# Samples among the last attention chunks, a third cache buffer, the sink's share by a small exp, rope's sum read from PSUM, and a scheduler that knows a shared port

## The chip, the cores and the metric

The kernel runs on one core of one Trainium2 chip. The metric is device time in microseconds (us); lower is better. The engines are TensorE (PE in the profile), VectorE (DVE), ScalarE (ACT), GpSimd (POOL) and SyncE (SP, which here only issues DMA). SBUF is the core's memory of 128 partitions, PSUM the accumulators in eight banks, which PE writes.

## The reference, cut to what matters

One inference step of a model of two layers: 512 prompt tokens, and eight samples of eight new tokens each (64 more), width 1024, all in float32.

```python
# layer 0: recurrent block (RNN), then SwiGLU          (FFN0)
x = x + g1 * recurrent_block(modulate(rms_norm(x, g), sh1, sc1))
x = x + g2 * swiglu(modulate(rms_norm(x, g), sh2, sc2))
# keys and values, once, from the stream after layer 0 (kv)
k, v = split(modulate(rms_norm(x, g), shk, sck) @ w_kv);  k = rope(k)
# layer 1: sliding-window attention with sinks, then SwiGLU (FFN1)
q = rope(h @ w_q)                                     # 16 heads of 64, 4 of k and v
s = (q @ k.T) * HEAD_DIM ** -0.5                      # in blocks of 128, window 128
m = maximum(max(s), sink)
e = exp(s - m)
p = e / (sum(e) + exp(sink - m))
x = x + g1 * ((p @ v) @ w_o)
x = x + g2 * swiglu(...)
y = rms_norm(x, final_g)
```

`apply_partial_rope` turns the first 16 elements of each head: `x1*cos - x2*sin`, `x2*cos + x1*sin`. A sample attends to its cache of 128 keys and to its own eight tokens.

## The kernel before, in words

**Data.** The 576 tokens are handled in two halves, A (`h = 0`) and B (`h = 1`), each of 256 prompt tokens and four samples of eight: `HC` = 288 columns. Features lie on partitions, tokens on columns. A product in float32 is made of three fp32r products, with the weights and the activations split in a high and a low part. One output tile of 128 features is 24 matmuls of 128x288 into one PSUM bank; an evacuation function then takes it from there.

**Order.** The code does not issue instructions. Each call on an engine is recorded (`Engine.record`, `Recorder.add`), which is why every instruction of the profile has the line L422. `Recorder.schedule` (L211) then simulates the engines with an estimated cost for each operation (L373 on) and the handover times of `DELAY` (L355), and takes on each engine, among the next 24 steps that are ready, the one with the smallest start plus 0.75 of its priority. Priority is the program order, within a window `WIN`. A switch of ACT's function table costs 2500 in that key. What comes out is a fixed order for each engine. Tiles come from pools: six PSUM banks `mm`, two `ada`, and the SBUF pools `sl` (37), `ta` (7), `tb` (8), `td` (4) of a few hundred columns each; a step that needs a tile waits for one to come free.

**Stages.** RNN, its output projection, FFN0, kv, attention, FFN1, final norm. Within the attention stage the list `ATT` (L53) sets the program order: `q6B` is the q projection of chunk 6 in half B, `a6B` the attention of that chunk (two heads by two blocks of 128 queries), `s1B` the attention of the second sample of half B, `fB` the end of attention (`attn_fin`), `o0B` an output projection. What comes behind `o2A` follows in its natural order.

**A q projection** ends in `evac_q` (L1492) with `rope` (L1426): DVE shuffles the bank into `t`, DVE multiplies the bank by the cosine table into `u`, POOL multiplies `t` by the sine table, and POOL adds both into the tile of q. The projection of keys, `evac_k`, uses `rope` as well, with two sums, for prompt and samples.

**An attention chunk** (`attn_chunk`, L1530) makes the scores on PE in two banks. DVE adds the mask and takes the row maximum into `ta`/`tb`; POOL writes the sink times 8 into one more column; ACT takes the exp over the scores and that column, with the sum; DVE the reciprocal; DVE and POOL scale two of the four blocks each. `second()`, which runs behind the next chunk's first part, transposes them on PE, copies them to `td` and multiplies with the values into an `ada` bank.

**A sample** (`attn_sample`, L1605) loads its cache rows (two DMAs on SP) into one of two buffers, transposes the keys on PE, and goes through the same steps with 160 columns. Its product with the cached values adds into a bank that the four samples of a half share (`OS`); the fourth one adds the product with the samples' own values.

Of the kernel before, what the change touches and what calls it, by code (L numbers as in the profile page):

```python
# [15 lines left out]
AF = mybir.ActivationFunctionType  # L16
# [36 lines left out]
ATT = ("q0A q1A a0A q0B q2A q1B a1A a0B q3A a1B q4A q2B a2A q3B a2B q5A q4B a3A q6A a3B a4A q5B "  # L53
       "a4B a5A q7A q6B a5B s0A a6A q7B s1A s2A s3A fA a7A a7B a6B s0B o0A s1B o1A s2B s3B fB o2A")
# [30 lines left out]
class Op:  # L85
    __slots__ = ("i", "prio", "eng", "emit", "cost", "func", "preds", "succ", "npred", "ready", "allocs", "start", "end", "done", "lat", "tiles", "_n")
# [42 lines left out]
class Recorder:  # L129
# [11 lines left out]
    @contextmanager  # L141
    def together(self):

        self.batch = []
        yield
        b, self.batch = self.batch, None

        def emit():
            for x in b:
                x[1]()  # L150

        self.add(b[0][0], emit, sum(x[2] for x in b), [y for x in b for y in x[3]], [y for x in b for y in x[4]])
# [22 lines left out]
    def add(self, eng, emit, cost, outs, ins, func=None, lat=0):  # L175
        if self.batch is not None:
            self.batch.append((eng, emit, cost, outs, ins))
            return
# [3 lines left out]
        op.eng, op.emit, op.cost, op.func, op.lat = eng, emit, cost, func, lat  # L182
        op.preds, op.succ, op.allocs, op.tiles = set(), [], [], set()
# [27 lines left out]
    def schedule(self):  # L211
# [18 lines left out]
        cold = 0.0  # L230
        pos = {n: j for k in self.order for j, n in enumerate(self.order[k])}
# [40 lines left out]
        while n_left:  # L272
# [7 lines left out]
            for e in engs:  # L280
# [3 lines left out]
                for pr, i, op in avail[e]:  # L284
# [10 lines left out]
                    s = max(f, op.ready, at)  # L295
                    sw = e == "ACT" and op.func and op.func not in FREE_FUNCS and (table[0] is None or op.func not in TABLES[table[0]][1])
# [25 lines left out]
            cost = op.cost  # L322
            if e == "PE":
                if s - free[e] > 3400:
                    cold = s + 3400
                if s < cold:
                    cost *= 2
# [36 lines left out]
class Engine:  # L364
# [8 lines left out]
    def record(self, name, args, kw):  # L373
# [11 lines left out]
        func, lat = None, 0  # L385
        if name == "matmul":
# [5 lines left out]
            if dt == F32 and 64 in (first.ap[0][1], args[1].ap[0][1]) and n >= P:  # L392

                cost = n * 2 / 2.4 + 20
            if first.ap[0][1] == 32 and args[1].ap[0][1] == P and n >= P:
                cost = n / 2.4 + 30 if dt == F32 else n / 9.6 + 15
        elif name == "transpose":
# [24 lines left out]
        self.rec.add(eng, lambda: getattr(obj, name)(*map(real, args), **{k: real(v) for k, v in kw.items()}), cost, outs, ins, func, lat)  # L422
# [26 lines left out]
def trunk_kernel(ctx, tc, a):  # L449
# [956 lines left out]
    def sink_setup():  # L1406
        sinks, sink8, nsink, sinkS = snk[:, 0:16], snk[:, 16:32], snk[:, 32:48], snk[:, 48:51]
        A["sink8"], A["nsink"], A["sinkS"] = sink8, nsink, sinkS
        sk = a["attn_sinks"][0]
        Q.dma_start(sinks.rearrange("p (g j l) -> p g j l", g=2, j=2), sk.partition_broadcast(P).rearrange("p (g j l) -> p g j l", g=2, j=2))  # L1410
# [3 lines left out]
        sv = sinks.rearrange("p (g j l) -> p g l j", g=2, j=2)  # L1414
        V.tensor_scalar(sink8.rearrange("p (g l j) -> p g l j", g=2, l=4)[:, 0], sv[:, 0], 8.0, None, ALU.mult)
        V.tensor_scalar(sink8.rearrange("p (g l j) -> p g l j", g=2, l=4)[:, 1], sv[:, 1], 8.0, None, ALU.mult)
        V.tensor_scalar(nsink.rearrange("p (g l j) -> p g l j", g=2, l=4)[:, 0], sv[:, 0], -1.0, None, ALU.mult)
        V.tensor_scalar(nsink.rearrange("p (g l j) -> p g l j", g=2, l=4)[:, 1], sv[:, 1], -1.0, None, ALU.mult)
# [111 lines left out]
    def attn_chunk(c):  # L1530
# [3 lines left out]
        def run(h):  # L1534
# [12 lines left out]
            masks, sink8, nsink = A["masks"], A["sink8"], A["nsink"]  # L1547
            for b, W in enumerate(wide):
                i = slice(2 * b, 2 * b + 2)
                for j in range(2):  # L1550
# [3 lines left out]
                    G.tensor_copy(y[:, W : W + 1], sink8[:, 2 * c + j : 2 * c + j + 1])  # L1554
                V.scalar_tensor_tensor(nm[:, i], mx[:, i], -0.125, nsink[:, 2 * c : 2 * c + 2], ALU.mult, ALU.min)
                for j in range(2):
                    y = e[b][j].f[:, 0 : W + 1]
                    S.activation(y, y, AF.Exp, bias=nm[:, 2 * b + j : 2 * b + j + 1], scale=0.125, accum_out=den[:, 2 * b + j : 2 * b + j + 1])
            V.reciprocal(rd, den)
            for b, W in enumerate(wide):  # L1560
                for j in range(2):
                    y, r = e[b][j].f[:, 0:W], rd[:, 2 * b + j : 2 * b + j + 1]
                    if b == j:
                        V.tensor_scalar(y, y, r, None, ALU.mult)
                    else:
                        G.tensor_tensor(y, y, r.to_broadcast([P, W]), ALU.mult)
# [394 lines left out]
```

## Time and profile before

| | |
|---|---|
| runs | 1310.57, 1307.85, 1308.14 us; median 1308.14 |
| profiled execution | 1308.17 us, of it the trace's span 1306.4 us |
| mean granted clock of PE | 0.986 |
| matmul records | 9532 |
| ACT busy, share | 643.8 us, 49% |
| HBM read, written | 160.85 MB, 4.87 MB |

The profile is one execution of the program. A row of a group names line, engine, operation, the output's and the input's tile, and the shapes; buffer numbers are left out there. `wh` are weights and other large tiles, `reg` constant areas, `h` the activations that a projection reads, `sl`, `ta`, `tb`, `td` the pools above. The granted clock is a share of full speed. A row of the timeline is one instruction or a group of like ones, with the idle time of its engine ahead of it and the instruction that ended it. PE's records overlap a little, so their starts tell more than their lengths.

### The profile page before, as it was taken

The numbers are of one execution on the slowest core, as the hardware profiler recorded it, in microseconds if no ns is written. First come the engines' busy times: TensorE is split into PE (matmuls) and PEld (weight loads), VectorE is DVE, ScalarE is ACT, GpSimd is POOL, SyncE is SP. The second block draws the span as 40 slices with busy tenths as digits, with TensorE's granted clock in tenths as the row PEclk, the third lists the DMA queues.
The fourth block names the chain that finished last, engine by engine and source line by source line (L and its number), as shares of the span: only waits on it lengthen the run. The fifth ranks groups of instructions, "written<-read, shape, count | busy, mean of one in ns | idle before, by whom it ended". The sixth has DMA issues, their size and how long they took to land. (4 is left out here: it accounts for less than half of the span.)

```text
span 1306.4 us, 25463 instructions
## 1 busy us (share of the span) xinstructions
PE 1256.6 (96%) x9532; PEld 1174.2 (90%) x9532; DVE 917.1 (70%) x2106; ACT 643.8 (49%) x1419; POOL 527.8 (40%) x813
## 2 busy tenths in 40 slices
PE   6998989999999999999998998999999999999997
PEld 5787889998999999999988886899999999999997
DVE  6986885697467547746688776457975875785767
ACT  4786873574245325424457555437642552552433
POOL 3465451224255145325246678201323633542422
PEclk8998999999999999999999999899999999999999
DMA  9963536325644735554342120233142332233232
GB/s 306 311 207 113 188 124 187 109 93 182 206 148 135 241 122 161 170 186 130 113 97 63 43 66 15 82 106 125 49 130 65 98 98 81 82 105 90 65 98 73
DMA packets 223981, 165.40 MB, mean 127 GB/s; under 512 B 23757, under 2 KB 209065, under 8 KB 223826
## 3 DMA queue, kind: packets, MB, share of 16 engines
q1 hardware_dynamic: 223410, 163.45, 41.1%
q8 instruction: 75, 1.23, 0.4%
q14 instruction: 48, 0.39, 0.1%
q0 software_dynamic: 448, 0.32, 0.1%
HBM read 160.85 MB, written 4.87 MB: 127 GB/s over the span
## 5 line engine op out<-in xcount | busy, mean ns | idle before, releaser
L422 PE MATMUL mm<-h,wh 128*128 128x288 f32 x4128 | 598.3, 299 | 10.8 <-ACT ta L422 3.7
L422 PEld LDWEIGHTS mm<-h,wh 128*128 128x128 f32 x4128 | 561.9, 189 | 32.7 <-issue 11.1
L422 PE MATMUL mm<-sl,wh 128*128 128x288 f32 x3218 | 460.0, 296 | 2.1 <-DVE wh L422 2.1
L422 PEld LDWEIGHTS mm<-sl,wh 128*128 128x128 f32 x3218 | 436.5, 188 | 8.8 <-PE ada L422 3.4
L422 ACT CAST wh<-raw 128x512 fp32r<-128x512 f32 (+2 forms) x388 | 266.9, 710 | 302.6 <-PE mm L422 231.6
L422 DVE TENSOR_TENSOR wh<-raw,wh 128x512 fp32r<-128x512 f32 (+2 forms) x388 | 358.3, 945 | 55.4 <-ACT wh L422 51.7
L422 POOL TENSOR_TENSOR raw<-raw 128x512 f32<-128x512 f32 x76 | 111.3, 1466 | 189.0 <-DVE wh L422 188.8
L422 DVE SCALAR_TENSOR_TENSOR x<-mm,mods,x 128x256 f32<-128x256 f32 x160 | 77.1, 482 | 147.8 <-PE mm L422 147.5
L422 POOL TENSOR_TENSOR x<-x,ta 128x32 f32<-128x32 f32 x152 | 57.6, 379 | 298.0 <-DVE ta L422 297.8
L422 POOL TENSOR_TENSOR raw<-raw,raw 128x512 f32<-128x512 f32 x76 | 111.8, 1473 | 3.3
L422 PE MATMUL mm<-tb,wh 128*128 128x288 f32 (+1 forms) x488 | 90.2, 298 | 6.1 <-POOL tb L422 2.8
L422 PEld LDWEIGHTS mm<-tb,wh 128*128 128x128 f32 x488 | 72.6, 188 | 10.9 <-POOL tb L422 3.5
L422 POOL TENSOR_TENSOR td<-td,td 128x288 f32<-128x288 f32 x38 | 33.1, 872 | 111.1 <-ACT td L422 105.7
L422 ACT COPY td<-mm 128x256 f32<-128x256 f32 (+1 forms) x102 | 34.1, 353 | 45.8 <-PE mm L422 41.1
L422 PE MATMUL mm<-ta,wh 128*128 128x288 f32 (+1 forms) x254 | 56.2, 298 | 0.0
L422 DVE TENSOR_TENSOR td<-mm,td 128x288 f32<-128x288 f32 x76 | 33.5, 452 | 31.7 <-PE mm L422 31.3
L422 ACT ACTIVATE ta<-x 128x288 f32<-128x288 f32 x56 | 24.8, 444 | 56.5 <-POOL x L422 53.4
L422 PE MATMUL ada<-reg,cz 128*32 128x512 f32 (+1 forms) x448 | 49.5, 553 | 0.0
L422 DVE TENSOR_TENSOR sl<-ta,sl 128x288 fp32r<-128x288 f32 x54 | 43.4, 806 | 3.8 <-ACT sl L422 3.4
L422 PEld LDWEIGHTS mm<-ta,wh 128*128 128x128 f32 x254 | 41.6, 188 | 2.5 <-issue 0.8
L422 ACT COPY ta<-mm 128x288 f32<-128x288 f32 (+1 forms) x50 | 18.9, 378 | 36.2 <-PE mm L422 36.1
L422 DVE TENSOR_TENSOR sl<-td,sl 128x288 fp32r<-128x288 f32 x50 | 34.3, 686 | 3.1 <-ACT sl L422 3.1
(198 smaller groups left out, 1287.0 us busy)
## 6 DMA issues: line engine op xcount, KB each, us to landing
raw<-in_ffn_w_in_dram SPq DMA_DIRECT2D x88, 512.0 KB
reg<-in_ada_w_dram SPq DMA_DIRECT2D x80, 512.0 KB
raw<-in_ffn_w_out_dram SPq DMA_DIRECT2D x48, 384.0 KB
raw<-in_rnn_w_in_dram SPq DMA_DIRECT2D x16, 512.0 KB
reg<-in_kv_ada_w_dram SPq DMA_DIRECT2D x16, 512.0 KB
wh<-in_ada_w_dram SPq DMA_DIRECT2D x24, 256.0 KB
raw<-in_rnn_w_out_dram SPq DMA_DIRECT2D x8, 512.0 KB
raw<-in_ffn_w_out_dram SPq DMA_DIRECT2D x16, 256.0 KB
```

The lines of the kernel that those rows point to most:

```text
L422: self.rec.add(eng, lambda: getattr(obj, name)(*map(real, args), **{k: real(v) for k, v in kw.items()}), cost, outs, ins, func, lat)
```

## The change

It has six parts.

1. `ATT`: a chunk follows its q projection one projection later than before in most places, and the samples stand among the last chunks.
2. Three cache buffers in place of two: the sample with `b % 3 == 2` uses the free half of `KT[1]` (`wh277` below).
3. The sink's share of the sum is no longer a column of the exp: DVE adds `nm + sink` (two values for each block), ACT takes one small exp over the four, DVE adds it to the sums. Of the four blocks ACT scales two (`j == 0`), POOL and DVE one each. The samples keep the column.
4. `rope` multiplies the bank by the cosines in place, and DVE, not POOL, adds POOL's product to it, out of the bank. The tile `u` is gone.
5. The scheduler holds that operations of POOL and those of DVE that read two SBUF inputs exclude each other (`port`), that PE needs 100 ns between matmuls of different shapes of array use (`mode`), and some costs are changed.
6. The setup of the sinks is written for part 3.

```diff
-ATT = ("q0A q1A a0A q0B q2A q1B a1A a0B q3A a1B q4A q2B a2A q3B a2B q5A q4B a3A q6A a3B a4A q5B "
-       "a4B a5A q7A q6B a5B s0A a6A q7B s1A s2A s3A fA a7A a7B a6B s0B o0A s1B o1A s2B s3B fB o2A")
+ATT = ("q0A q1A a0A q0B q2A a1A q1B a0B q3A a2A q2B a1B q4A a3A q3B a2B q5A a4A q4B a3B q6A a5A q5B a4B q7A a6A s0A q6B a5B s1A "
+       "a7A s2A q7B s3A s0B a6B fA s1B o0A s2B a7B s3B o1A fB o2A")
...
                     s = max(f, op.ready, at)
+                    if op.port:
+                        s = max(s, port - 130)
+                    if e == "PE" and op.mode != mode:
+                        s = max(s, f + 100)
...
+            if op.port:
+                port = s + cost
+            if e == "PE":
+                mode = op.mode
...
+        wide = [x for x in ins if not _is_psum(x) and not str(x.space).endswith("DRAM") and (_free(x) > 1 or f == 1)]
+        port = eng == "POOL" and name != "dma_start" and bool(wide) or eng == "DVE" and not ps_ and (len(wide) > 1 or name == "tensor_scalar" and f > 1)
...
-            cost, lat = (460.0 if eng == "SP" else 1020.0), n * 4 / 360.0 + 5
+            cost, lat = (460.0 if eng == "SP" else 1020.0), n * 4 / 335.0 + 5
...
+            elif name == "tensor_tensor_scan":
+                cost = 70 + 2.1 * f
...
-                cost = 67 + (1.2 if name == "tensor_tensor" and not ps_ and f >= 288 else 1.0417) * f + (61 if scal and name == "scalar_tensor_tensor" else 0)
+                cost = 67 + 1.0417 * f + (61 if scal and name == "scalar_tensor_tensor" else 0)
...
-                cost = 145 + (165 if ALU.pow in vals else 2.6) * f
+                cost = 150 + (165 if ALU.pow in vals else 2.4) * f
...
     def rope(h, o, outs):
-        t, u = ta(), tb()
+        t = ta()
         tabs = A["tabs"]
         V.stream_shuffle(t.f[:, 0:HC], o[:, 0:HC], SHUF)
-        V.tensor_tensor(u.f[:, 0:HC], o[:, 0:HC], tabs[h][:, 0, :], ALU.mult)
         G.tensor_tensor(t.f[:, 0:HC], t.f[:, 0:HC], tabs[h][:, 1, :], ALU.mult)
+        V.tensor_tensor(o[:, 0:HC], o[:, 0:HC], tabs[h][:, 0, :], ALU.mult)
         for cs, dst in outs:
-            G.tensor_tensor(dst, u.f[:, cs], t.f[:, cs], ALU.add)
+            V.tensor_tensor(dst, o[:, cs], t.f[:, cs], ALU.add)
         t.done()
-        u.done()
...
-                    G.tensor_copy(y[:, W : W + 1], sink8[:, 2 * c + j : 2 * c + j + 1])
                 V.scalar_tensor_tensor(nm[:, i], mx[:, i], -0.125, nsink[:, 2 * c : 2 * c + 2], ALU.mult, ALU.min)
+                V.tensor_tensor(mx[:, i], nm[:, i], sinks[:, 2 * c : 2 * c + 2], ALU.add)
                 for j in range(2):
-                    y = e[b][j].f[:, 0 : W + 1]
+                    y = e[b][j].f[:, 0:W]
                     S.activation(y, y, AF.Exp, bias=nm[:, 2 * b + j : 2 * b + j + 1], scale=0.125, accum_out=den[:, 2 * b + j : 2 * b + j + 1])
+            S.activation(mx, mx, AF.Exp)
+            V.tensor_tensor(den, den, mx, ALU.add)
             V.reciprocal(rd, den)
             for b, W in enumerate(wide):
                 for j in range(2):
                     y, r = e[b][j].f[:, 0:W], rd[:, 2 * b + j : 2 * b + j + 1]
-                    if b == j:
+                    if j == 0:
+                        S.activation(y, y, AF.Copy, scale=r)
+                    elif b == 0:
+                        G.tensor_tensor(y, y, r.to_broadcast([P, W]), ALU.mult)
+                    else:
                         V.tensor_scalar(y, y, r, None, ALU.mult)
-                    else:
-                        G.tensor_tensor(y, y, r.to_broadcast([P, W]), ALU.mult)
...
-            ck, cv = cache[:, b % 2, 0, :], cache[:, b % 2, 1, :]
+            ck, cv = [KT[1].f[:, 512 + 256 * i : 768 + 256 * i] if b % 3 == 2 else cache[:, b % 3, i, :] for i in range(2)]
```

The program has 8972 matmuls before and after; DVE's instructions go from 2088 to 2143, ACT's from 1346 to 1395, POOL's from 818 to 715, and ACT loads a table 22 times in both.

The first place is PE's order behind the last q projection, q7B (`mm351` before, `mm361` after), and ahead of the first output projection (`mm381` before, `mm382` after). In the names `reg109` is the cache, `reg110` the samples' q, `wh276` the keys, `ident` marks a transpose, a row `64x160` is half of a sample's scores, and `128x64 x2` is a sample's product with its cached values, into the shared bank `mm342` (`mm341` after). Before, with q7B long done, the scores of s1A, s2A and s3A stand here in one piece:

```order
L422 MATMUL mm353_10399<-ta308_10307,reg110_7018 64x160
L422 MATMUL mm353_10399<-tb154_10309,reg110_7018 64x160
L422 MATMUL mm358_10419<-ta310_10311,reg110_7018 64x160
L422 MATMUL mm358_10419<-tb155_10314,reg110_7018 64x160
L422 MATMUL mm361_10435<-ta312_10350,reg110_7018 64x160
L422 MATMUL mm361_10435<-tb156_10353,reg110_7018 64x160
L422 MATMUL mm359_10448<-ident_66,ta309_10390 128x128
L422 MATMUL mm359_10448<-ident_66,ta309_10390 32x128
L422 MATMUL mm362_10459<-ident_66,ta311_10396 128x128
L422 MATMUL mm362_10459<-ident_66,ta311_10396 32x128
L422 MATMUL mm342_10298<-td107_10454,reg109_9780 128x64 x2
```

After, the scores of s1A and the transposed keys of s2A, out of the third buffer, stand just ahead of q7B, and the first sample's product inside it:

```order
L442 MATMUL mm352_10206<-ta307_9446,reg110_7017 64x160
L442 MATMUL mm352_10206<-tb134_9450,reg110_7017 64x160
L442 MATMUL mm350_10217<-ident_66,ta303_9408 128x128
L442 MATMUL mm350_10217<-ident_66,ta303_9408 32x128
L442 MATMUL mm359_10225<-ident_66,wh277_9768 128x128 x2
L442 MATMUL mm361_10230<-h14_8893,wh298_9371 128x288 x2
L442 MATMUL mm361_10230<-h14_8893,wh299_9704 128x288
L442 MATMUL mm361_10230<-h14_8893,wh298_9371 128x288
L442 MATMUL mm341_10245<-td102_10235,reg109_9633 128x64 x2
```

Behind q7B there stand now the scores of s2A, later those of s3A and of s0B; from the first row of this piece to the first output projection, `mm382`, it is 37 rows:

```order
L442 MATMUL mm366_10435<-ta314_10350,reg110_7017 64x160
L442 MATMUL mm366_10435<-tb138_9658,reg110_7017 64x160
L442 MATMUL mm370_10440<-ta316_10392,reg110_7017 64x160
L442 MATMUL mm370_10440<-tb139_10203,reg110_7017 64x160
L442 MATMUL mm396_10404<-ident_66,wh276_8572 128x128
L442 MATMUL mm363_10452<-ident_66,ta309_10376 128x128
```

The second place is the same engine in the third output projection of half A (`mm398`), behind the samples: the scores of chunk a7B (`mm386`, `mm387`) stand there now, and their transposes 35 matmuls later inside `mm399`. Before, they stood ahead of the first output projection. The first of the two pieces below is that of the scores:

```order
L442 MATMUL mm398_10731<-h05_10059,wh304_10134 128x288 x2
L442 MATMUL mm386_10763<-wh276_8572,sl255_10348 128x256
L442 MATMUL mm387_10765<-wh276_8572,sl255_10348 128x256
L442 MATMUL mm386_10763<-wh276_8572,sl255_10348 128x256
L442 MATMUL mm387_10765<-wh276_8572,sl255_10348 128x256
L442 MATMUL mm398_10731<-h05_10059,wh305_10247 128x288
```

The third place is ACT's order in the RNN stage, where the gelus (`ta39`, `ta44`, `ta45`, out of the banks `mm44`, `mm49`, `mm52`) need a table of their own. Before, three stand in a row behind one load:

```order
L422 CAST ta60_1641<-sl38_1569 128x300
L422 ACT_TABLE_LOAD
L422 ACTIVATE ta39_1655<-mm44_1291 128x288
L422 ACTIVATE ta44_1659<-mm49_1402 128x288
L422 ACTIVATE ta45_1665<-mm52_1541 128x288
L422 CAST sl29_1672<-ta39_1655 128x288
```

After, the gelu of `mm44` stands among the earlier gates, and that of `mm49` ahead of a load which comes for the next exps; the third, of `mm52`, is left behind a load of its own some 20 rows later:

```order
L442 ACTIVATE sl33_1415<-ta43_1403,sp2_83 128x300
L442 CAST ta50_1422<-sl27_1298 128x300
L442 CAST wh33_1442<-raw17_1033 128x1024
L442 ACTIVATE ta44_1452<-mm49_1399 128x288
L442 ACT_TABLE_LOAD
L442 ACTIVATE sl26_1469<-ta38_1220,nsp4_84 128x300
L442 ACTIVATE sl32_1479<-ta41_1347,nsp4_84 128x300
```

More of the change, by code (lines that the diff above doesn't have):

```diff
@@ L85 @@
 class Op:
-    __slots__ = ("i", "prio", "eng", "emit", "cost", "func", "preds", "succ", "npred", "ready", "allocs", "start", "end", "done", "lat", "tiles", "_n")
+    __slots__ = ("i", "prio", "eng", "emit", "cost", "func", "preds", "succ", "npred", "ready", "allocs", "start", "end", "done", "lat", "tiles", "port", "mode")
 class Ref:
@@ L150, in emit @@
                 x[1]()
-        self.add(b[0][0], emit, sum(x[2] for x in b), [y for x in b for y in x[3]], [y for x in b for y in x[4]])
+        self.add(b[0][0], emit, sum(x[2] for x in b), [y for x in b for y in x[3]], [y for x in b for y in x[4]], mode=self.mode)
     def tile(self, pool, kind, cap, reserve, shape, dt, name):
@@ L173, in regions, with add @@
         return [(ap.tensor.name, p0, p0 + ap.ap[0][1], (o + st * i) * size, (o + st * i + n) * size) for i in range(c)]
-    def add(self, eng, emit, cost, outs, ins, func=None, lat=0):
+    def add(self, eng, emit, cost, outs, ins, func=None, lat=0, port=False, mode=0):
         if self.batch is not None:
+            self.mode = mode
             self.batch.append((eng, emit, cost, outs, ins))
@@ L182, in add @@
         op.eng, op.emit, op.cost, op.func, op.lat = eng, emit, cost, func, lat
+        op.port, op.mode = port, mode
         op.preds, op.succ, op.allocs, op.tiles = set(), [], [], set()
@@ L230, in schedule @@
         cold = 0.0
+        port, mode = 0.0, 0
         pos = {n: j for k in self.order for j, n in enumerate(self.order[k])}
@@ L385, in record @@
         func, lat = None, 0
+        wide = [x for x in ins if not _is_psum(x) and not str(x.space).endswith("DRAM") and (_free(x) > 1 or f == 1)]
+        port = eng == "POOL" and name != "dma_start" and bool(wide) or eng == "DVE" and not ps_ and (len(wide) > 1 or name == "tensor_scalar" and f > 1)
+        mode = 0
         if name == "matmul":
@@ L392, in record @@
             if dt == F32 and 64 in (first.ap[0][1], args[1].ap[0][1]) and n >= P:
+                mode = 1 if args[1].ap[0][1] == 64 else 2
                 cost = n * 2 / 2.4 + 20
@@ L396, in record @@
                 cost = n / 2.4 + 30 if dt == F32 else n / 9.6 + 15
+                mode = 3
         elif name == "transpose":
@@ L421, in record @@
                 cost = 120 + 3.3 * min(f, 32) + max(f - 32, 0) * 1.1
-        self.rec.add(eng, lambda: getattr(obj, name)(*map(real, args), **{k: real(v) for k, v in kw.items()}), cost, outs, ins, func, lat)
+        self.rec.add(eng, lambda: getattr(obj, name)(*map(real, args), **{k: real(v) for k, v in kw.items()}), cost, outs, ins, func, lat, port, mode)
 class Slots:
@@ L1406, in sink_setup @@
     def sink_setup():
-        sinks, sink8, nsink, sinkS = snk[:, 0:16], snk[:, 16:32], snk[:, 32:48], snk[:, 48:51]
-        A["sink8"], A["nsink"], A["sinkS"] = sink8, nsink, sinkS
+        raw, sinks, nsink, sinkS = snk[:, 0:16], snk[:, 16:32], snk[:, 32:48], snk[:, 48:51]
+        A["sinks"], A["nsink"], A["sinkS"] = sinks, nsink, sinkS
         sk = a["attn_sinks"][0]
-        Q.dma_start(sinks.rearrange("p (g j l) -> p g j l", g=2, j=2), sk.partition_broadcast(P).rearrange("p (g j l) -> p g j l", g=2, j=2))
+        Q.dma_start(raw.rearrange("p (g j l) -> p g j l", g=2, j=2), sk.partition_broadcast(P).rearrange("p (g j l) -> p g j l", g=2, j=2))
         for hh in range(16):
             Q.dma_start(sinkS[hh * 8 : hh * 8 + 8, 0:1], sk[hh : hh + 1].partition_broadcast(8))
[L1414 to L1418, printed above, removed]
+        sv = raw.rearrange("p (g j l) -> p g l j", g=2, j=2)
+        for g in range(2):
+            V.tensor_copy(sinks.rearrange("p (g l j) -> p g l j", g=2, l=4)[:, g], sv[:, g])
+            V.tensor_scalar(nsink.rearrange("p (g l j) -> p g l j", g=2, l=4)[:, g], sv[:, g], -1.0, None, ALU.mult)
         V.tensor_scalar(sinkS[:, 1:2], sinkS[:, 0:1], 8.0, None, ALU.mult)
@@ L1546, in run @@
             e = [(ta(), tb()) for _ in range(2)]
-            masks, sink8, nsink = A["masks"], A["sink8"], A["nsink"]
+            masks, sinks, nsink = A["masks"], A["sinks"], A["nsink"]
             for b, W in enumerate(wide):
```

## The prediction

> **What bounds the kernel now.** I read the page first: the 40 slices of PE and the busy totals.
>
> ```profile
> PE   6998989999999999999998998999999999999997
> PE 1256.6 (96%) x9532; PEld 1174.2 (90%) x9532; DVE 917.1 (70%) x2106; ACT 643.8 (49%) x1419; POOL 527.8 (40%) x813
> ```
>
> TensorE is busy 1256.6 of 1306.4 us, every other engine 70% or less. An edit that takes work from DVE, ACT or POOL is worth only what it takes from the other 49.8 us, or from places where PE's granted clock is low. The change adds and removes no matmul. So the second view is the windows, cut where the stages and the low slices of PE lie (columns: stretch and its length, busy us of PE, weight loads, DVE, ACT, POOL with their instructions, granted clock, DMA share, GB/s).
>
> ```profile
> 0.00:65.00 65.00, 52.16 (x495) 39.67 (x496) 51.29 (x199) 39.30 (x91) 25.91 (x57) 0.95 1.01 308
> 98.00:131.00 33.00, 27.13 (x187) 24.97 (x187) 22.50 (x46) 20.32 (x44) 17.48 (x42) 0.90 0.34 112
> 653.00:719.00 66.00, 59.49 (x427) 55.42 (x425) 55.29 (x143) 44.63 (x104) 34.73 (x54) 1.00 0.36 81
> 719.00:798.70 79.70, 79.69 (x670) 69.13 (x669) 60.77 (x234) 44.20 (x146) 57.49 (x131) 1.00 0.17 45
> 798.70:828.80 30.10, 23.94 (x141) 16.69 (x139) 17.69 (x74) 17.87 (x69) 17.97 (x53) 0.72 0.25 73
> 828.80:1274.00 445.20, 442.42 (x3318) 436.27 (x3319) 308.18 (x595) 195.35 (x411) 155.62 (x170) 1.00 0.30 89
> ```
>
> FFN1, from 828.8, leaves PE 2.8 us idle in 445, and the slices of FFN0 (229 to 653) read nine throughout: nothing is to be won there. The start is bound by DMA (share 1.01), and the change touches neither it nor the final norm. Most of the attention stage, 719 to 798.7, has PE at 79.69 of 79.70. What the change can win lies in its **tail**, 798.7 (end of the last q projection, q7B) to 828.8, and a little in the RNN stage (98 to 131) and the kv stage (653 to 719), where the scheduler's new costs shift the order.
>
> The tail cut along the clock's own steps, with the waits on its path from PE's timeline (start, us, instruction, in brackets the idle time before it and its releaser):
>
> ```profile
> 801.50:804.90 3.40, 1.61 (x11) 1.28 (x12) 1.37 (x4) 3.40 (x16) 3.26 (x8) 1.00 0.15 42
> 804.90:808.40 3.50, 3.50 (x25) 2.22 (x23) 1.64 (x2) 1.70 (x5) 3.50 (x5) 0.51 0.06 11
> 811.80:815.20 3.40, 1.59 (x14) 0.61 (x10) 2.46 (x16) 1.10 (x5) 2.46 (x13) 1.00 0.00 0
> 815.20:818.60 3.40, 3.08 (x14) 2.38 (x14) 3.12 (x21) 2.97 (x13) 0.86 (x4) 0.50 0.12 40
> 818.60:822.00 3.40, 2.55 (x12) 1.83 (x11) 1.99 (x10) 0.93 (x4) 1.19 (x5) 0.50 0.53 165
> 822.00:825.40 3.40, 3.40 (x12) 2.44 (x12) 1.99 (x10) 1.66 (x8) 1.43 (x3) 0.50 0.65 193
> 825.40:828.80 3.40, 3.40 (x22) 2.76 (x21) 1.77 (x6) 2.44 (x10) 0.72 (x3) 0.50 0.55 154
> ```
>
> ```profile
> 802.23 0.66 PE L422 MATMUL mm<-td,reg 128*128 128x64 f32 x4 [0.96 <-DVE td L422]
> 803.95 0.33 PE L422 MATMUL mm<-ident,ta 128*128 128x128 f32 x1 [1.06 <-ACT tb L422]
> 811.50 0.32 PE L422 MATMUL mm<-ta,reg 128*64 128x160 f32 x1 [0.45 <-ACT reg L422]
> 812.52 0.32 PE L422 MATMUL mm<-ta,reg 128*64 128x160 f32 x1 [0.52 <-DVE stat L422]
> 815.52 0.66 PE L422 MATMUL mm<-ident,ta 128*128 128x128 f32 x2 [0.56 <-DVE stat L422]
> 815.97 0.96 PE L422 MATMUL mm<-td,reg 128*128 128x64 f32 x4
> 821.26 0.45 PE L422 MATMUL mm<-ident,ta 128*128 128x128 f32 x1 [0.85 <-DVE ta L422]
> 822.60 2.07 PE L422 MATMUL mm<-wh,reg 32*128 32x256 f32 x4
> 826.65 0.61 PE L422 MATMUL mm<-h,wh 128*128 128x288 f32 x1
> ```
>
> The rows tell one story. After q7B no dense product is left until o0A at 826.65. Only four samples' short steps and the last chunks remain, each a chain PE, DVE or ACT, POOL, PE. The idle time is 30.10 - 23.94 = 6.16 us. After a window in which PE was busy 1.6 of 3.4 us (801.5, 811.8) the clock is 0.50: 3.50 + 3.08 + 2.55 + 3.40 + 3.40 = 15.93 us ran at half clock, which costs half, 7.97. Together the tail loses **14.1 us**. The work itself would take 23.94 - 7.97 = 16.0 us at full clock, of which some 1.1 (2.15 at half) is already o0A: 14.9 us of short work.
>
> The Trainium skill, "TensorE: Matmul & The Clock Gate", Part 1, says that the gate halves the clock after about one idle window of 3.4 us, in free-running windows. The trace agrees on the halving and the length, not on idle: here the longest wait ahead of the fall at 804.9 was 1.06 us. By the page, remaining short waits would cost only themselves and the sum below would be 1.7 us less; by the rows, they can still halve a window. The sum goes by the rows.
>
> **The change part by part.**
>
> *Order and third cache buffer.* The list now lets the samples follow among the last chunks. Before, all sample scores but the first stand behind q7B. After, the scores of s0A and s1A, the key transposes of s2A (from the third buffer, wh277, so they need not wait for s0A's last product) stand ahead of it. The two programs list 69 rows each between q7B's end and o0A, so the work there stays near 14.9 us; what shrinks are chains. The longest one left is s3A's: from scores at 811.50 to its product at 815.97 a sample took 4.47 us. Then come that product (0.66, row 802.23), the product with the samples' own values (1.12 at full clock, below), and from its end to o0A 826.65 - (822.60 + 2.07) = 1.98: 8.2 us. Behind s3A's scores stand 35 of the 69 rows, by that share 7.5 us of work. So 0.7 us wait. I add three short waits in order, at the mean of the six bracketed ones above (4.40 / 6 = 0.73), 2.2, and one window at half clock, 3.4 / 2 = 1.7, since the after-order still has stretches of nothing but short steps. 4.6 us remain of 14.1: **-9.5**. Bounds: -13.4 with only the 0.7 wait, -5.3 if the four half windows from 815.2 stay (12.43 / 2 = 6.2, plus 2.6 of waits left).
>
> ```profile
> 787.06 3.45 PE L422 MATMUL mm<-h,wh 128*128 128x288 f32 x24
> 790.44 1.13 PE L422 MATMUL mm<-wh,sl 64*128 64x256 f32 x8
> 796.92 0.27 PE L422 MATMUL mm<-ident,ta 128*128 128x128 f32 x1
> 847.52 1.12 PE L422 MATMUL mm<-wh,reg 32*128 32x256 f32 x4
> ```
>
> With each sample its two cache loads move up on SP, and its copies and one scaling on POOL go past chunk a6A's. The DMA share is 0.17 from 719 to 798.7 and POOL is busy 57.49 of 79.7 there, with 35 us less to do after the change (below): these cost nothing.
>
> *What the order pays.* Chunk a7B now has its scores inside o2A and its transposes 35 dense matmuls later. At (790.44 - 787.06) / 24 = 0.141 each that is 4.9 us of cover. A chunk before took 796.92 - 791.57 = 5.35 from scores to first transpose. The sink's new small steps (an ACT exp, a DVE add) are of the kinds that cost 0.2 us, with a handover each, some 0.65: 6.0. **+1.1** (0 to 2.5, the upper end if a queue holds the longer chain once more for as long).
>
> *Sink and normalisation.* The groups by form, 719 to 850 us (busy, mean ns, idle before):
>
> ```profile
> L422 POOL TENSOR_TENSOR sl<-tb,ta 128x288 f32<-128x288 f32 x15 | 12.1, 811 | 0.5
> L422 POOL COPY ta<-snk 128x1 f32<-128x1 f32 x35 | 6.6, 193 | 3.7 <-PE mm L422 3.2
> L422 POOL TENSOR_TENSOR ta<-ta,stat 128x256 f32<-128x256 f32 x16 | 10.2, 638 | 0.1
> L422 DVE TENSOR_SCALAR tb<-tb,stat 128x256 f32<-128x256 f32 x16 | 9.6, 602 | 0.0
> L422 DVE TENSOR_TENSOR tb<-mm,reg 128x288 f32<-128x288 f32 x14 | 6.2, 440 | 0.1
> L422 DVE SCALAR_TENSOR_TENSOR stat<-stat,snk 128x2 f32<-128x2 f32 x32 | 6.4, 200 | 0.2
> L422 ACT CAST h<-sl 128x256 fp32r<-128x256 f32 x13 | 4.7, 406 | 0.4 <-DVE sl L422 0.4
> ```
>
> Per chunk POOL loses four copies of 0.19 and one of two wide scalings (0.64), and the rope's add (0.81): 0.77 + 0.64 + 0.81 = 2.2 us, 35 over 16 chunks. ACT gains two scalings (as its 128x256 cast, 0.41) and one small exp (0.2, as a small operation): 1.0, 16 in all. DVE gains three small adds (0.2 each) and the rope's sum (0.44, like its multiply from PSUM), loses one scaling (0.60): +0.44, 7 in all. Over the 79.7 us before q7B's end ACT stands at 44.20 and DVE at 60.77, so neither becomes the bound, and PE's own 79.69 hides all of it: **0**. Without that cover it would be the longer chain, 0.65 a chunk, 10 in all.
>
> *Rope's sum from PSUM.* DVE's sum now waits for POOL's product, and the bank is free only behind it. Behind the waiting sum on DVE stand the next chunk's reductions of scores, and for these ACT's exps wait. The hold grows by up to 0.81 + 0.44 = 1.25 us. From 719 to 798.7 some 76 tiles go through six banks, a mean hold of 6 x 79.7 / 76 = 6.3 us allowed, and PE waits nowhere. I take **0**; the upper end is a rival below. In the kv stage eight adds of keys go to DVE, four wide and four narrow, 4 x (0.44 + 0.2) = 2.6 us on an engine with 55.29 of 66 busy; POOL loses as much. 0, from -2 to +2.6.
>
> *The scheduler's costs.* They move rows in the RNN stage. The two worst stretches, and the rows that end their waits:
>
> ```profile
> 105.00:112.00 7.00, 3.51 (x26) 1.51 (x18) 6.41 (x10) 0.99 (x3) 6.75 (x14) 1.00 0.46 141
> 112.00:119.00 7.00, 4.62 (x19) 4.62 (x20) 3.47 (x15) 5.20 (x11) 1.06 (x3) 0.51 0.42 162
> 110.19 0.71 PE L422 MATMUL mm<-ident,ta 128*128 128x128 f32 x4 [2.40 <-ACT ta L422]
> 114.38 5.47 PE L422 MATMUL mm<-h,wh 128*128 128x288 f32 x24 [3.47 <-ACT ta L422]
> 112.62 1.28 ACT L422 ACT_TABLE_LOAD   x1
> ```
>
> Lost here: 3.49 + 2.38 idle, and 4.62 x 0.49 = 2.26 by the clock, 8.1 us. Three gelus stood together behind one table load (the order's rows above), while their products held three of the six banks; in the new program two of them stand before it, among earlier steps, so PE has banks left. Against it: the two loads now stand closer to DVE's casts of the next weights, and PE waits for those. I take not the 8.1 nor 0, but the one wait that those banks end, 3.47, less a margin for the weights: **-3** (0 to -6).
>
> **Sum**, from the profiled execution, 1308.17 us (span 1306.4 and 1.77 around it; the median of the three runs is 1308.14, so no shift): 1308.17 - 9.5 + 1.1 - 3.0 = **1296.8**.
>
> **The rivals.**
>
> *R1, the tail's clock stays low.* Fewer waits, but steps too short to bring the clock back: 822.0 and 825.4 were busy throughout and still at 0.50. Then the tail wins 5.3 in place of 9.5: 1301.0. Against it: the window at 819 had gaps, and 808.4 to 815.2 was at full clock with short steps. The Trainium skill, same page, Part 4, says that transposes do not count as PE busy in the same way; the tail is mostly transposes, so by it this rival would be the likelier. The rows 822.0 and 825.4 do not contradict it.
>
> *R2, slower: banks held by rope.* Each q projection's bank is freed 1.25 us later. If PE comes to that bank before it is free, it waits: 16 x 1.25 = 20 us over all, 1316.8. It turns the change slower from 13.9 us on (the 11.4 won, and 2.6 for the measurement): 11 of the 16. Against it stand six banks, and 79.69 busy of 79.70.
>
> *R3, the change does not do what it says.* The same 69 rows stand between q7B and o0A. If the waits move to the chunks that come later, in o0A and o1A, and the RNN term is nothing, the time stays at 1308.
>
> **How the numbers follow.** The forecast has 0.63, R1 0.17, R3 0.10, R2 0.10. The low end is 1308.17 - 13.4 - 6, 1288.8, which I round to 1288; the high end takes in R1 with the RNN term at nothing and half of the kv stage's 2.6, 1305.3, say 1306. R3 and R2 stay outside. About 0.2% (2.6 us) is what a measurement of this kernel can tell from no change: faster is forecast and R1, less a sliver, 0.79; same is R3 and that sliver, 0.11; slower is R2, 0.10.
>
> **What would show it.** In the tail: q7B's end to o0A about 18 to 20 us in place of 27.95, at most one window at 0.50, and waits in brackets under 1 us. A chunk's transposes after o0A with a wait near 1 us. In the RNN stage at 105 to 119, PE with under 5 us lost. Wrong would be: brackets ahead of the projections 719 to 798 released by DVE with tile mm (R2), four windows at 0.50 in the tail (R1), or new waits of some 9 us behind o0A (R3). In every case PE's idle time in both FFN stages stays where it is.

## The result, and the profile after

The change made the kernel faster by more than was forecast: a median of 1288.01 us (four runs, 1285.66 to 1290.79) against 1309.36 before (four runs, 1307.85 to 1311.75), a ratio of 0.9836 with a 95% interval of 0.9808 to 0.9864. The forecast was 1296.8 us with 1288 to 1306 as its range, worked out from the profiled execution of before, 1308.17 us. The profiled execution of after took 1286.79 us (span 1285.0), which lies below that range, as does the ratio on 1308.17, 1286.7. The sign was right, but 21.4 us were won where the sum had 11.4.

The page after, its PE slices and busy totals:

```profile
PE   7898999999999999999999999999999999999997
PE 1247.7 (97%) x9532; PEld 1176.5 (92%) x9532; DVE 891.7 (69%) x2161; ACT 655.9 (51%) x1468; POOL 485.7 (38%) x710
```

The low slice of the tail is gone, POOL has 42 us less to do, ACT 12 more. DVE has 55 instructions more and yet 25 us *less*. That is the first hint of a term that was missing.

To see where the 21.4 us went, take the n-th matmul of shape 128x288 in each trace (each has 7992 of them) and subtract its start before from its start after. The difference at some n, with the start before in us:

```
n (start before)      after - before
 300   (93.6)   +1.8   front of RNN
1350  (275.9)   -0.2   in FFN0
3900  (646.5)   -0.3   end of FFN0
4200  (695.3)   -0.5   kv
4350  (720.9)   -5.1   first q projections
4650  (795.1)   -1.0   last q projection
4800  (857.5)  -15.0   output projections
4950  (877.5)  -15.0   start of FFN1
7650 (1244.5)  -21.2   end of FFN1
```

So the stretch from kv to the start of FFN1, attention for short, gave 14.7 us and FFN1 6.2. The windows after, with the same columns as those shown of before, cut at the same matmuls (from the first kv projection to the first q projections, n = 4500 to 4650, n = 4650 to 4800, FFN1, and q7B's end to o0A):

```profile
677.40:717.60 40.20, 40.20 (x293) 39.72 (x293) 35.79 (x103) 33.39 (x80) 19.84 (x23) 0.96 0.27 58
750.90:794.10 43.20, 41.44 (x367) 36.19 (x367) 36.66 (x159) 33.10 (x118) 19.41 (x41) 1.00 0.18 53
794.10:842.50 48.40, 45.94 (x369) 39.36 (x368) 28.78 (x123) 29.26 (x105) 14.76 (x36) 0.96 0.28 81
862.40:1223.30 360.90, 360.90 (x2721) 360.19 (x2720) 249.34 (x477) 166.03 (x344) 141.40 (x140) 1.00 0.31 91
796.79:815.88 19.09, 16.63 (x134) 12.07 (x134) 14.16 (x66) 15.34 (x57) 10.73 (x27) 0.91 0.30 86
```

The first four of these stretches in before:

```profile
676.20:718.10 41.90, 37.70 (x265) 34.75 (x264) 37.12 (x94) 31.22 (x79) 25.82 (x35) 1.00 0.34 71
755.00:795.00 40.00, 40.00 (x350) 34.20 (x349) 30.75 (x118) 25.18 (x85) 30.92 (x67) 1.00 0.18 54
795.00:857.50 62.50, 56.29 (x392) 45.96 (x393) 34.91 (x142) 29.70 (x106) 24.62 (x72) 0.86 0.24 70
877.50:1244.50 367.00, 364.27 (x2720) 360.94 (x2720) 263.36 (x477) 167.02 (x344) 142.06 (x140) 1.00 0.30 89
```

Ahead of and among the first q projections PE had 4.2 us idle and has none; 28 more records stand there, and the clock of 0.96 costs about 1.6. In the tail (795.0 to 857.5 before) PE lost 6.21 us idle and 0.14 x 56.29 = 7.9 by its clock; after, 2.46 and 0.04 x 45.94 = 1.8. That is 9.8 us less lost, and q7B's end to o0A fell from 27.94 to 19.09 us. One long wait remains there, with one window of 3.41 us at half clock behind it, and the clock is full again before o0A:

```profile
806.19 0.32 PE L442 MATMUL mm<-ta,reg 128*64 128x160 f32 x1 [2.12 <-ACT sl L442]
807.55:810.96 3.41, 3.41 (x22) 2.44 (x21) 3.00 (x17) 2.67 (x11) 1.19 (x4) 0.50 0.21 55
813.60:817.00 3.40, 3.40 (x26) 2.70 (x26) 2.38 (x10) 2.21 (x8) 0.65 (x5) 1.00 0.62 177
```

In FFN1 the surprise: 367.0 us became 360.9 for 2720 and 2721 matmul records. Only 2.73 us of that was idle time in the window's row; the other 3.4 stood inside PE's busy time, 364.27 against 360.90. The groups by form in FFN1, before and then after, show which engine it was (columns: busy us, mean ns, idle before and releasers):

```profile
L422 PE MATMUL mm<-tb,wh 128*128 128x288 f32 x204 | 36.5, 300 | 2.3 <-DVE td L422 1.3 <-DVE wh L422 0.8
L422 DVE TENSOR_TENSOR sl<-ta,sl 128x288 fp32r<-128x288 f32 x16 | 17.8, 1113 | 0.6 <-ACT sl L422 0.5
```

```profile
L442 PE MATMUL mm<-tb,wh 128*128 128x288 f32 x204 | 35.6, 296 | 0.0
L442 DVE TENSOR_TENSOR sl<-ta,sl 128x288 fp32r<-128x288 f32 x16 | 7.4, 464 | 0.8 <-ACT sl L442 0.8
```

The same DVE operation of the same shape takes 1113 ns before and 464 after. The timeline of before shows what one of the slow ones did (start, us, instruction, idle time before it):

```profile
955.58 1.39 POOL L422 TENSOR_TENSOR raw<-raw 128x512 f32<-128x512 f32 x1
955.74 1.54 DVE L422 TENSOR_TENSOR sl<-ta,sl 128x288 fp32r<-128x288 f32 x1
957.20 0.68 DVE L422 TENSOR_TENSOR wh<-raw,wh 128x512 fp32r<-128x512 f32 x1
957.80 0.44 DVE L422 TENSOR_TENSOR td<-mm,td 128x288 f32<-128x288 f32 x1
958.30 0.66 PE L422 MATMUL mm<-tb,wh 128*128 128x288 f32 x3 [1.26 <-DVE td L422]
```

DVE's add of two SBUF tiles starts 0.16 us into a POOL operation and ends 0.3 us after it. DVE's queue behind it is late, and PE waits 1.26 us for the step after the next. In the whole trace of before 21 such adds of the FFN stages met no POOL operation and took about 0.45 us; 17 began inside one of POOL's operations on `raw` and took about 1.52.

### The profile page after: what moved, and what is told of

Its sections match the earlier page's. It is cut to its first block, busy times and chain, and to the rows that moved or that the text cites. A ratio compares the mean times of both kernels' runs of the same rounds, so it can differ in the third digit from the quotient of the medians.

```text
span 1285.0 us, 25432 instructions
## 1 busy us (share of the span) xinstructions
PE 1247.7 (97%) x9532; PEld 1176.5 (92%) x9532; DVE 891.7 (69%) x2161; ACT 655.9 (51%) x1468; POOL 485.7 (38%) x710
## 4 chain that ended last, share of the span: by engine, by line
PE 80%; DVE 8%; ACT 5%; POOL 2%; DMA 2%; issue 2%; SPq 1%; ACTq 0%; DVEq 0%; POOLq 0%
PE mm L442 76%; PE ada L442 4%; DVE sl L442 2%; DVE wh L442 2%; DVE ta L442 1%; POOL sl L442 1%; DMA raw<-in_ffn_w_in_dram 1%; DVE tb L442 1%; ACT tb L442 1%; ACT sl L442 1%; ACT wh L442 1%; ACT h L442 1%; SPq L442 1%; DMA reg<-in_x_prompt_dram 1%; ACT L442 1%
## 5 line engine op out<-in xcount | busy, mean ns | idle before, releaser
L442 DVE TENSOR_TENSOR wh<-raw,wh 128x512 fp32r<-128x512 f32 (+2 forms) x388 | 346.4, 914 | 54.7 <-ACT wh L442 50.1
L442 POOL TENSOR_TENSOR x<-x,ta 128x32 f32<-128x32 f32 x152 | 53.5, 352 | 305.6 <-DVE ta L442 305.5
L442 ACT ACTIVATE ta<-ta,stat 128x256 f32<-128x256 f32 (+2 forms) x72 | 32.3, 470 | 21.4 <-DVE stat L442 21.1
L442 DVE TENSOR_TENSOR sl<-td,sl 128x288 fp32r<-128x288 f32 x50 | 39.1, 782 | 6.0 <-ACT sl L442 5.4
L442 DVE TENSOR_TENSOR ta<-ta,mm 128x288 f32<-128x288 f32 x38 | 17.2, 453 | 28.8 <-PE mm L442 28.8
```

## The experiments

Each row is one kernel's lag behind before at the same matmuls (us; negative is earlier), the time between n = 4950 and 7650 (FFN1), and the ratio of its runs to before with its interval. The labels are those of the paragraphs below. Two kernels were traced twice, which shows how far single traces scatter: after and e12 differ by at most 0.7 us, e8 and e11 by up to 2.3, of which some 1.7 is a half-clock window of 3.4 us that e8 has in its tail (from 804.7) and e11 has not.

```
       n=1350  3900  4350  4650  4800  7650   FFN1  ratio
before    0     0     0     0     0     0    367.0
after   -0.2  -0.3  -5.1  -1.0 -15.0 -21.2   360.8  0.9836 [0.9808, 0.9864]
e1      -1.4  -0.8  -2.7  +3.8 -10.7 -11.1   366.6  0.9920 [0.9904, 0.9936]
e2      -2.8  -4.7  -7.7  -5.9  -5.8 -11.0   361.9  0.9913 [0.9896, 0.9930]
e3      -0.1  +0.2  -0.3  +1.1  -0.9  -7.1   360.9  0.9931 [0.9912, 0.9950]
e4      +1.0  +1.3  +2.5 +10.2  +2.2  +2.3   367.0  1.0013 [1.0001, 1.0024]
e5      +1.4  +1.8  -0.1  +0.5  -3.8  -3.6   367.2  0.9949 [0.9930, 0.9969]
e6      +2.0  +2.2  +2.9  +8.0  -6.1  -6.3   366.8  0.9947 [0.9929, 0.9965]
e7      -1.3  -0.9  +0.5  +5.8  -7.7  -8.0   366.8  0.9949 [0.9931, 0.9968]
e8      -2.1  -4.0  -6.2  -1.8 -17.1 -22.6   361.5  0.9824 [0.9804, 0.9845]
e9      +2.5  +2.9  +4.3  +6.7  -6.8  -7.2   366.6  0.9927 [0.9913, 0.9941]
e10     +0.3  +1.3  -4.6  -0.9  -9.8 -15.7   361.2  0.9878 [0.9865, 0.9891]
e11     -3.0  -4.8  -7.1  -2.7 -19.4 -24.9   361.6  0.9821 [0.9808, 0.9833]
e12     -0.3  +0.4  -4.5  -0.4 -14.7 -20.9   360.8  0.9849 [0.9836, 0.9861]
```

**Where FFN1's time came from: e1, e2, e3.** e1 is the changed kernel with the scheduler of before:

```diff
-                    if op.port:
-                        s = max(s, port - 130)
-                    if e == "PE" and op.mode != mode:
-                        s = max(s, f + 100)
...
-            cost, lat = (460.0 if eng == "SP" else 1020.0), n * 4 / 335.0 + 5
+            cost, lat = (460.0 if eng == "SP" else 1020.0), n * 4 / 360.0 + 5
...
```

(with the other costs put back too).

> The changed kernel with the scheduler of before (no port, no mode term, the old costs); the list, the third buffer, the sink and rope stay new. Theory T1 (the FFN1 gain of 6 us comes from the port term, which keeps DVE's adds of two SBUF tiles out of POOL's): FFN1 takes some 376 us again between its milestones in place of 370, the add sl<-ta,sl of 128x288 about 0.8 to 1.1 us in place of 0.46, total near 1294. Rival T2 (FFN1 runs faster because attention leaves it another state: tiles, loads, order): FFN1 stays at 370, total near 1288. The tail from q7B's end to o0A stays at 19 to 21 us by both.

The 370 and 376 us of the expectations are FFN1 cut some 9 us longer, 360.8 and 367.0 in this document. e1 took 1298.2 us. FFN1 is back at 366.6, and the add at 1124 ns, just above T1's range. T2 falls: attention left FFN1 in the new state, and FFN1 did not run faster. T1's total of 1294 was missed by 4 us, since attention lost 4.8 as well (-9.9 from n = 3900 to 4800, after -14.7). The tail did not stay at 19 to 21 us either: q7B's end to o0A is 15.60 (803.85 to 819.45).

```profile
866.80:1233.40 366.60, 363.80 (x2721) 360.51 (x2720) 263.68 (x477) 167.05 (x344) 141.84 (x140) 1.00 0.31 90
L436 DVE TENSOR_TENSOR sl<-ta,sl 128x288 fp32r<-128x288 f32 x16 | 18.0, 1124 | 0.5 <-ACT sl L436 0.5
```

e2 is the kernel before with the `port` term alone, e3 with all of the new scheduler; the kernel's own instructions are those of before in both.

```diff
+                    if op.port:
+                        s = max(s, port - 130)
...
```

In the code the term covers more than the change's list says: of DVE not only operations with two SBUF inputs, but also its scalings (`tensor_scalar`) of a wide SBUF tile.

> The kernel before with the port term of the scheduler alone. T1: FFN1 370 us, sl<-ta,sl near 0.46 us, total near 1302. T2: FFN1 376 us, total 1308. The tail stays near 28 us by both.

> The kernel before with the whole scheduler of after (port, mode, costs). T1: like the port alone, FFN1 370 us, and whatever mode and costs add in the small steps: 1300 to 1302. T2: 1308. If the mode term is what shortens PE's small work in attention (6 us less full-clock busy time for the same matmuls), another 3 to 5 us go between kv and o0A: near 1297.

e2 took 1297.22 us, more than T1 said was to be had: FFN1 gives 5.2, and another 4.7 come before the end of FFN0 and 3.0 in the first q projections, of which attention gives 1.9 back. The add takes 454 ns, and the tail stays, at 28.51 us.

```profile
871.60:1233.50 361.90, 361.60 (x2720) 360.42 (x2719) 243.55 (x477) 165.29 (x343) 139.83 (x138) 1.00 0.31 90
L438 DVE TENSOR_TENSOR sl<-ta,sl 128x288 fp32r<-128x288 f32 x16 | 7.3, 454 | 4.7 <-ACT sl L438 4.7
```

e3 took 1299.43 us: about the same FFN1 gain, but only 1.1 us for attention (n = 3900 to 4800), and the front of the program is 2.8 us late at n = 300. The expectation that the mode term would shorten attention fell. Over all fourteen traces here FFN1 takes 360.8 to 361.9 us with the port term (seven traces) and 366.6 to 367.2 without it (seven), whatever else differs.

**Where attention's time came from: e4 to e7.** e4 is the kernel before with the new list and the third buffer, my prediction's main term by itself.

```diff
+ATT = ("q0A q1A a0A q0B q2A a1A q1B a0B q3A a2A q2B a1B q4A a3A q3B a2B q5A a4A q4B a3B q6A a5A q5B a4B q7A a6A s0A q6B a5B s1A "
...
-            ck, cv = cache[:, b % 2, 0, :], cache[:, b % 2, 1, :]
+            ck, cv = [KT[1].f[:, 512 + 256 * i : 768 + 256 * i] if b % 3 == 2 else cache[:, b % 3, i, :] for i in range(2)]
```

> The kernel before with the new list ATT and the third cache buffer alone. My prediction's main term: the tail shrinks from 28 us by 8 to 10, total near 1299. T1: FFN1 stays at 376. T2: FFN1 falls to 370 as in after, total near 1293.

It won nothing: 1310.21 us, a ratio just above 1. Both theories had a wrong total. The tail did shrink, by 8.0 us from n = 4650 to 4800, but the stretch from 4350 to 4650, where PE had waited for nothing before, grew by 7.7. And q7B's end to o0A fell by 4.1 us only, from 27.94 to 23.84, not by the 8 to 10 that I expected. The windows of those q projections, before and then e4, and e4's from q7B's end to o0A:

```profile
721.00:795.00 74.00, 73.99 (x627) 63.82 (x626) 55.61 (x205) 41.77 (x137) 53.85 (x123) 1.00 0.17 46
```

```profile
723.50:805.00 81.50, 78.38 (x657) 65.95 (x655) 68.57 (x242) 48.52 (x158) 58.75 (x132) 1.00 0.28 67
810.74:834.58 23.84, 20.52 (x129) 13.49 (x127) 13.56 (x61) 15.31 (x55) 14.74 (x43) 0.86 0.28 80
```

In the q projections DVE has 18% more instructions and 23% more busy time. Of the 7.5 us PE is idle for 3.1, mostly released by ACT's and DVE's steps of the chunks; in the other 4.4 it is busy, with 30 more records, so that part of the growth is work that came forward out of the tail. DVE's scalings of a 128x256 tile `ta` took 787 ns there (row at e9), against 669 in the same window of before:

```profile
L422 DVE TENSOR_SCALAR ta<-ta,stat 128x256 f32<-128x256 f32 x5 | 3.3, 669 | 0.1
```

So e5 to e7 asked which of the other parts the list needs: e5 is the sink, its scalings and rope with the old list and two buffers, e6 the new list with rope, e7 the new list with the sink and its scalings, all with the old scheduler. The edits are those of the diff above for these functions.

> The kernel before with the new sink, normalisation and rope, with the old list, two buffers and the old scheduler. Alone, the new list with its buffer (the run before this) moved its attention stretch (dense matmul 4350 to 4800) only from 136.5 to 136.2 us, though the same list with the new sink and rope had 128.6. Theory I (sink and rope take the load off POOL that the new list needs, neither pays alone): 135 to 137 us here and total near 1308. Rival A (the 8 us are the sink's and rope's own, the list is worth nothing): 128 to 130 us and total near 1300.

> The kernel before with the new list, third buffer and the new rope; the sink as before, the old scheduler. If rope's add off POOL (0.81 us each) is what the list needs: the attention stretch near 130 us, total near 1302. If it is the sink's part: near 136, total 1308 to 1310.

> The kernel before with the new list, third buffer and the new sink and normalisation; rope as before, the old scheduler. If the sink's part (four copies and one scaling a chunk off POOL, 1.4 us) is what the list needs: the attention stretch near 130 us, total near 1302. If it is rope: near 136, total 1308 to 1310.

They took 1302.38, 1301.53 and 1302.5 us. In the expectations' own cut (n = 4350 to 4800) before has 136.5 us, e4 136.2, e5 132.9, e6 127.5, e7 128.3 and e1 128.6. Theory I fell in half: e5 lies between it and rival A. Sink and rope win 5.6 us with the old list (n = 3900 to 4800), so they pay alone. Of this nothing comes from the q projections in between (4350 to 4650: 0.6 later). 1.9 come ahead of them and 4.2 behind them, in the tail, where q7B's end to o0A is 20.82 us without the new list and buffer:

```profile
799.22:820.04 20.82, 17.23 (x115) 11.18 (x113) 15.30 (x74) 15.13 (x59) 9.96 (x22) 0.83 0.27 78
```

The 4.2 us are more than single traces scatter by, the 0.6 and the 1.9 are not.

e6 and e7 both came out as their first branch said, so neither rope nor the sink is the one part that the list needs. Either of them makes the list pay: from 3900 to 4800 it is +0.9 for the list alone, -8.3 with rope, -6.8 with the sink, -9.9 with both (e1), and -14.7 with the scheduler too. The parts do not add: +0.9 and -5.6 are not -9.9. Between e4 and e1, which differ by sink, scalings and rope alone, 6.4 of the 10.8 us lie in the tail, 3.1 ahead of and among the first q projections, and 1.2 between 4350 and 4650.

**What the sink's copies cost: e9.** The kernel of e4, with the 64 copies of the sinks on ACT:

```diff
-                    G.tensor_copy(y[:, W : W + 1], sink8[:, 2 * c + j : 2 * c + j + 1])
+                    S.copy(y[:, W : W + 1], sink8[:, 2 * c + j : 2 * c + j + 1])
```

> The kernel before with the new list and third buffer, where ACT and not POOL makes the 64 copies of the sinks; nothing else of the sink, rope or scheduler is new. Theory C (POOL's small operations hold the port that DVE's steps need, and the new list has no slack for it): DVE's small 128x2 step falls from 0.35 us to 0.2, the loss in the first part of attention (dense matmul 4350 to 4650) falls from 7.7 us to 4 or less, total 1303 to 1306. Rival D (what helps is the small exp and the split of the scaling, not POOL's load): the same 7 to 8 us loss, total 1309 to 1311, as ACT has 13 us more.

It took 1297.2 us for moving 64 copies of one column from one engine to another. That is 13 us below e4, but the two ran on different chips; by their ratios to before it is about 11, and 9.5 between the profiled executions (e9's runs spread from 1295.1 to 1300.92). From 3900 to 4800 it is -9.7, and the loss from 4350 to 4650 falls from 7.7 to 2.4 us. D falls: neither the small exp nor the new split of the scalings is needed for it. C expected 1303 to 1306; it has its 4 us or less in that stretch and beat its total, but missed its row. The small 128x2 step still takes 337 ns. What fell is the scaling of `ta`, by 1.7 us in all, too little to be the gain; first e4's rows and then e9's:

```profile
L422 DVE SCALAR_TENSOR_TENSOR stat<-stat,snk 128x2 f32<-128x2 f32 x26 | 9.1, 349 | 0.1
L422 DVE TENSOR_SCALAR ta<-ta,stat 128x256 f32<-128x256 f32 x5 | 3.9, 787 | 0.1
```

```profile
L422 DVE SCALAR_TENSOR_TENSOR stat<-stat,snk 128x2 f32<-128x2 f32 x25 | 8.4, 337 | 0.1
L422 DVE TENSOR_SCALAR ta<-ta,stat 128x256 f32<-128x256 f32 x5 | 2.2, 445 | 0.2
```

That the list pays once these copies are off POOL is shown; that they are the only cause is not, since in e6 they stay on POOL and the list pays too. Whether they cost by the time they take in POOL's queue, ahead of the exps that need the column, or by DVE's steps that they hold up, the runs do not tell: moving them takes away both, and the schedule around them moves too.

**The third buffer: e10.** The changed kernel with two.

```diff
-            ck, cv = [KT[1].f[:, 512 + 256 * i : 768 + 256 * i] if b % 3 == 2 else cache[:, b % 3, i, :] for i in range(2)]
+            ck, cv = cache[:, b % 2, 0, :], cache[:, b % 2, 1, :]
```

> The changed kernel with two cache buffers in place of three. If the third buffer carries part of the tail's gain, as my prediction has it (s2A's keys need not wait for s0A's product): the time from q7B's end to o0A grows from 19 us by 2 to 4, total 1290 to 1292. If the list alone does it: within 1 us of the changed kernel, 1287 to 1289.

1291.69 us, as expected for the first theory, and 4.6 above the changed kernel on the same chip (e12). But its place was off: up to o0A it costs only about 1.2 us (817.57 - 797.15 = 20.42 from start to start of the two dense matmuls, against 19.23 in e12), not 2 to 4. The rest comes at and behind o0A: PE waits 1.12 us at 817.57 and 1.58 at 842.91, both times for ACT's `h`, and the clock is halved for 3.4 us from 817.7.

**The port alone: e8, e11, e12.** The changed kernel without the mode term and with the old costs.

```diff
-                    if e == "PE" and op.mode != mode:
-                        s = max(s, f + 100)
...
-                cost = 150 + (165 if ALU.pow in vals else 2.4) * f
+                cost = 145 + (165 if ALU.pow in vals else 2.6) * f
...
```

> The changed kernel with the port term alone of the new scheduler (no mode term, the old costs). Theory P (all that the scheduler gives is the port): RNN and FFN0 win some 5 us as in the kernel before with the port alone, FFN1 5 to 6, and attention 8 to 10: near 1286, not slower than the whole change. Rival (mode and costs give the rest of attention's gain): 1289 to 1292.

> The changed kernel with the port term alone, on the same chip as the changed kernel. If mode and costs are worth nothing or less: 2 us below the changed kernel, 1285 to 1286. If the earlier run was chance: 1288.

> The changed kernel again, for the comparison on one chip: 1287 to 1289.

e8 took 1285.59 us, as theory P had it, though attention gave 13.1 us and not 8 to 10. e11 is the same kernel again: 1284.02, a little below its range, beside e12's 1287.09 on the same chip. The ratios of e11 and e12 to before are 0.9821 [0.9808, 0.9833] and 0.9849 [0.9836, 0.9861]: without the mode term and the new costs the changed kernel is 3 us faster. The difference lies before the end of FFN0 (-4.8 against +0.4 at n = 3900).

## Why the prediction was right and wrong, point by point

**The tail** was right in size. The sum had 14.1 us lost there, of which 9.5 would be won; 9.8 were. "q7B's end to o0A about 18 to 20 us" came to 19.09, "at most one window at 0.50" to one. The one wait of 2.12 us, for the scores behind ACT's step, stands in place of the three of 0.73; it is over the "under 1 us" of the signs.

**But its cause was incomplete**, so that the size was partly luck. The prediction gave the tail to the list and the buffer, and cost sink, rope and scalings at 0, since "PE's own 79.69 hides all of it". That cover was there (e5 is 0.6 us later between n = 4350 and 4650), but it ends with q7B, and the sum did not ask what these edits do behind it. There, and ahead of the first q projections, they pay: alone 5.6 us in attention, 4.2 of them in the tail (e5). List and buffer alone bring q7B's end to o0A to 23.84 us and win nothing in all (e4). So the 0 for these edits was the first step that failed: alone they are worth 5.6 us in attention, and without them, or the copies moved as in e9, the list is worth nothing. Whether that is POOL's lighter load or the chunks' shorter chains, and through which wait, stays open.

**FFN1**, "nothing is to be won there", was the step that cost the range: 6.2 us. The 2.8 us of idle time were read as all that there was, and as staying ("PE's idle time in both FFN stages stays where it is"); in FFN1 it fell from 2.73 us to nothing. The waits of 0.1 to 0.25 us ahead of single matmuls do not show as idle, since the ends of matmuls are modelled: a record is about 0.295 us long and the starts lie 0.133 apart, so a start that is late by up to 0.16 us leaves no gap. 22 starts were late by 0.10 to 0.25 us in FFN1 before, 5 after. They do show as 0.9% more busy time for the same work (364.27 and 360.90), which only the comparison tells. The row that would have told it before was DVE's: one operation of one shape at 450 or at 1540 ns. The Trainium skill, "SBUF — State Buffer", section "SBUF: two separate sides", says that DVE and GpSimd share one pair of ports under an exclusive lock, that a DVE operation with two SBUF inputs needs it against a GpSimd operation that reads SBUF, that whichever starts first has them for its whole instruction, and that the other is blocked until then. The trace agrees: 0.45 us alone, about 1.52 begun inside POOL's operation. I had the scheduler's port term in the list of edits, and weighed it only by the rows that it moves in the RNN stage.

**The kv stage and the first q projections**, 0 with bounds of -2 and +2.6, gave -4.8 (n = 3900 to 4350). e5 has -1.9 there, e2 -3.0, together about the sum: rope and sink off POOL seem to be part of it, the port the rest. That split is not shown: e3, with the port too, has -0.5, and e8 and e11, with all of these edits, have -2.2 and -2.3.

**RNN**, -3: the mechanism was half right, and the sum wrong. The waits for the gelus are gone, and a wait for DVE's weights came in their place, as the sentence against it had it:

```profile
116.54 3.49 PE L442 MATMUL mm<-h,wh 128*128 128x288 f32 x13 [4.03 <-DVE wh L442]
```

With 4.03 us idle and a half clock from 114.64 to 121.47, in which PE was busy 4.93 us, 6.5 us are lost there in place of 8.1; the sign said under 5. From n = 300 to 1350 the trace gains 2.0, but the program was 1.8 us late by n = 300. The four traces with the mode term and the new costs (after, e3, e10, e12) are 1.7 to 3.4 late there, the other ten between 1.5 early and 1.6 late. And only those four have half-clock windows between 36 and 67 us, after from 60.03 to 66.86 with PE busy 6.03, which costs 3.0. So the late front goes with the mode term and the new costs; which of the two was not tried.

**a7B behind o0A**, +1.1, did not come: no wait over 0.15 us stands between 807 and 900 us after.

**The rivals.** R2, banks held by rope, did not come: no wait ahead of the q projections is released by DVE's `mm`. R1 did not: the half clock ended at 810.96, behind one fully busy window of transposes and short products, and the window from 813.6 is at full clock, with transposes in it. R3's total came in e4, where the list alone wins nothing, but not its mechanism: the new waits stand ahead of q7B, not behind o0A, where e4 has none over 0.15 us up to FFN1. With the rest of the change R3 did not come.

By terms: the tail as forecast, FFN1 -6.2 in place of 0, the first projections -4.8 in place of 0, RNN and FFN0 -0.3 in place of -3, a7B 0 in place of +1.1. From n = 4350 to 4650 the trace is 4.1 us later, since small steps stand there now that stood in the tail; the tail's count from n = 4650 to 4800, -14.0, includes them, and both together are -9.9.

## What to carry to other kernels

An engine that is never the bound can still be the loss, where its operations block those of another that feeds the bound: look for one operation of one shape with two durations, and for the other engine's instruction that covers the long ones. A stage with its bound engine at 99% busy is not thereby full; compare the time for one matmul with the best stage of the same shape. And a cost that is "hidden" is hidden only where the cover stands: ask what the same edit does in the stretches without it, and cost it together with the rearrangement that changes them.

## What the runs showed of the hardware that was not expected

A DVE add of two SBUF tiles of 128x288 takes 0.45 us alone and about 1.52 us if it begins inside a POOL operation on SBUF of 1.4 to 1.6 us: it ends 0.3 us behind that one (POOL until 956.97, DVE until 957.28), so some 0.15 of its own 0.45 us pass while it is blocked. Waits of 0.1 us ahead of matmuls are counted as PE busy, as records of 0.295 us whose starts lie 0.133 apart overlap. And a window need not be idle for the clock to fall behind it: after one in which PE was busy 1.36 of 3.41 us, with a longest wait of 2.12, the granted clock was 0.50. The Trainium skill, "TensorE: Matmul & The Clock Gate", Part 1, asks for an idle window; the trace differs, as it did before the change:

```profile
804.14:807.55 3.41, 1.36 (x12) 0.94 (x13) 1.86 (x12) 3.05 (x15) 1.86 (x9) 1.00 0.62 189
```
